# First chunks by pairs of input tiles, last job tile by tile, final stores on two queues

## The chip, the core and the metric

The kernel runs on one core of a Trainium2 chip. The metric is device time in microseconds (us) of one execution; shown are the median of several runs and one execution recorded by the hardware profiler. The engines are TensorE (PE for products, PEld for weight loads), VectorE (DVE), ScalarE (ACT), GpSimd (POOL) and SyncE (SP), which issues most DMAs.

## What is computed

One layer of a decoder trunk for 256 prompt tokens and 64 sample tokens (`NT` = 320 columns in all), width 2048, all in float32:

```python
x += 0.5 * SwiGLU_a(RMSNorm(x))    # w_ffa_in (2048 x 11264), w_ffa_out (5632 x 2048)
x += TokenMix(RMSNorm(x))          # mLSTM and dilated attention, w_in, w_pm, w_pa, w_out
x += 0.5 * SwiGLU_b(RMSNorm(x))    # w_ffb_in, w_ffb_out
y = RMSNorm(x)                     # final norm, written out for all tokens
```

Beside `y` the kernel returns attention rows and recurrent states; the change doesn't touch them.

## The kernel before

Activations are kept transposed: `X[j]` (j = 0 to 7) is a pair of tiles of 128 features by 320 tokens. Every matrix product is a job: 256 columns of a weight matrix, that is two halves `m` of 128, over all its input tiles. A job is cut into chunks of up to four input tiles, 512 KB of weights each. To keep float32 precision with faster products, a weight chunk `raw` is split into `hi` (ScalarE, line 223) and `lo` (VectorE, line 224), the moving operand likewise into `xh` and `xl`, and three products are summed in PSUM: `hi` by `xh`, `hi` by `xl`, `lo` by `xh` (line 144). `raw` has 4 buffers, `hi` and `lo` have 3 each.

The program order is written out by hand. `run_job` (line 270) goes through a job's chunks; ahead of each it splits chunks to come, takes one step of background generators (`every` at each chunk, `even` at every second), issues the loads to come, and then the chunk's products. Each engine works its instructions in this order. The evacuation of a job (`flush_evac`) runs in the first chunk of the next.

**Start.** The four `load_x` calls (512 columns of all tokens each, the prompt in one DMA and the sample tokens in another) alternate with the loads of weight chunks, all on SyncE's queue; six small vectors follow (`load_vecs`). `prep_pair(j)` (line 1494) transposes two 128-column tiles of x on TensorE, copies them to `X[j]`, and makes `XH[j]` (scaled, rounded) and `XL[j]` (the rest). `first_chunk` (line 1513) prepares pairs 0, 1 and 2 and splits chunk 0 ahead of the first product, with eight warming products on `ones`; the further pairs come between the halves of chunks 0 to 2. `first_sumsq` (line 1535) squares `X[0]` to `X[7]` on ScalarE in steps at chunks 2 to 5 and adds the squares into `ss` on VectorE (line 377); at chunk 6 `rstd_now` sums over features on TensorE (two products of `ones` by `ss`) and makes `rstd`, which the first evacuation needs. `init_tables` begins at the third chunk (its first `even` step comes at chunk 0 and only yields), `vec_table` at the fifth.

**End.** The last eight jobs make the final X pairs. `ffb_last` (line 1443) adds the job's result, squares it, scales by the final norm's weights (`xn`), and two chunks later transposes `xn` back and copies it into `Y` (128 x 3 x 2048). For the last job the sums over tokens (`token_sums`, line 1435) are taken in two parts, `ss` of pairs 0 to 6 during the job and `sq` of pair 7 behind it. Then `rt` (one factor a token) is made, and `Y` is scaled and stored in two halves of 1024 columns, three row tiles each (two of the prompt on 128 partitions, the sample rows on partitions 64 to 127), all six stores on SyncE's queue.

Of the kernel before, what the change touches and what calls it, by code (L numbers as in the profile page):

```python
# [128 lines left out]
def decoder_kernel(tc, I, O, K):  # L129
# [10 lines left out]
    def dma(out, in_):  # L140
        nc.sync.dma_start(out, in_)  # L141
# [128 lines left out]
    def run_job(job):  # L270
        cs, nkt, mov, evac, kind, setup = job
        ps = fg_tile()
        for n, (ci, k0, nk) in enumerate(cs):
            run_later()
            if ci < 5:
                first_chunk(ci, 0)
            else:
                split_upto(ci + HLB)
            if tick[0] % 2 == 0:
                step(even)  # L280
            else:
                step(odd)
            tick[0] += 1
            pace[0] += 8
            if pace[0] >= 15:
                pace[0] -= 15
                step(slow)
            step(every)
            if n == 0 and setup is not None:
                setup()  # L290
            if ci == 7 or (n == 0 and ci != 4):
                flush_evac()
            load_upto(ci + HLB + RAWB)
            h, l = wh.pop(ci), wl.pop(ci)
            for m in range(1 if kind == "mif" else 2):
                if m and ci < 3:
                    first_chunk(ci, 1)
                for k in range(nk):
                    xh, xl = mov(k0 + k)
                    if kind == "mif":  # L300
                        a, b, out = h[:, k], l[:, k], ps[0:64, 0, 0:NT]
                    else:
                        a, b, out = h[:, k, m * 128:(m + 1) * 128], l[:, k, m * 128:(m + 1) * 128], ps[:, m, 0:NT]
                    first, last = k0 + k == 0, k0 + k == nkt - 1
                    mm(out, a, xh, start=first, stop=False)
                    mm(out, a, xl, start=False, stop=False)
                    mm(out, b, xh, start=False, stop=last)
        pending[0] = (evac, ps)
# [58 lines left out]
                                   hi[:, m].bitcast(F32), op0=OP.mult, op1=OP.subtract)  # L367
        XH[j], XL[j] = hi, lo

    def sumsq(x, j, sq_pool):  # L370
        if j == 0:
            state["ss"] = sq_pool.tile([128, 2, NT], F32, tag="ss", bufs=1, name="ss")
            S.activation(state["ss"], x, AF.Square)
        else:
            sq = sq_pool.tile([128, 2, NT], F32, tag="ft", bufs=4, name="sq")
            S.activation(sq, x, AF.Square)
            V.tensor_tensor(state["ss"], state["ss"], sq, op=OP.add)

    def rstd_gen():
        yield  # L380
# [16 lines left out]
    X = {}  # L397
    S.dma_start(ident, K["ident"])
    vffa = fp.tile([16, 128], F32, name="vffa")
    S.dma_start(vffa, I["ln_ffa"].rearrange("o (k p) -> (o k) p", p=128))  # L400
    vrow = fp.tile([128, 2, 128], F32, name="vrow")
    xl = {}

    def load_x(c):
        xl[c] = fp.tile([128, 3, 512], F32, tag="xl", bufs=3, name="xl")
        G.memset(xl[c][64:128, 2], 0.0)
        dma(xl[c][:, 0:2], I["x_prompt"][0].rearrange("(t p) d -> p t d", p=128)[:, :, c * 512:(c + 1) * 512])
        dma(xl[c][0:NS, 2], I["x_sample"].rearrange("b t d -> (b t) d")[:, c * 512:(c + 1) * 512])

    def load_vecs():  # L410
        for r, nm in ((16, "ln_mix"), (32, "ln_ffb"), (48, "conv_b")):
# [989 lines left out]
    def ft_tile(name):  # L1401
        return pool_box["p"].tile([128, 2, NT], F32, tag="ft", bufs=4, name=name)
# [29 lines left out]

    TOK = (0, 128, NT - 128)

    def token_sums(x):
        ps = bg_tile()
        for t, t0 in enumerate(TOK):
            for m in range(2):
                mm(ps[:, t:t + 1], x[:, m, t0:t0 + 128], ones[:, 0:1], m == 0, m == 1)
        return ps  # L1440


    def ffb_last(ps, j):
        p = pool_box["p"]
        if j == 0:
            S.activation(epst2, epst, AF.Sqrt)
        if j < 7:
            V.scalar_tensor_tensor(X[j], ps[:, :, 0:NT], 0.5, X[j], op0=OP.mult, op1=OP.add)
            sumsq(X[j], j, p)
        else:  # L1450
            Y["sq"] = ft_tile("sq")
            for m in range(2):
                V.scalar_tensor_tensor(X[j][:, m], ps[:, m, 0:NT], 0.5, X[j][:, m], op0=OP.mult, op1=OP.add)
                S.activation(Y["sq"][:, m], X[j][:, m], AF.Square)
        xn = ft_tile("xn")
        for m in range(2):
            c = G_LF + 2 * j + m
            S.activation(xn[:, m], X[j][:, m], AF.Copy, scale=gv[:, c:c + 1])
        yield
        if j < 7:  # L1460
            yield
        if j == 6:
            pa_ = token_sums(state["ss"])
            V.tensor_copy(rt, pa_[:, 0:3])
        a, b = bg_tile(), bg_tile()
        for t in range(2):
            for m in range(2):
                tr(a[:, t * 256 + m * 128:t * 256 + (m + 1) * 128], xn[:, m, t * 128:(t + 1) * 128])
        for m in range(2):
            tr(b[:, m * 128:(m + 1) * 128], xn[:, m, NT - 128:NT])  # L1470
        if j == 0:
            Y["t"] = p.tile([128, 3, D], F32, name="Y")
        S.copy(Y["t"][:, 0:2, j * 256:(j + 1) * 256], a.rearrange("p (t c) -> p t c", t=2))
        V.tensor_copy(Y["t"][64:128, 2, j * 256:(j + 1) * 256], b[64:128, 0:256])

    ff_jobs(I["w_ffb_in"][0], I["w_ffb_out"][0], lambda: pool_box["p"], ffb_last)


    for c in range(4):
        load_x(c)  # L1480
        load_upto(c + 1)
    load_vecs()
    def warm(n):
        ps = bg_tile()
        for _ in range(n):
# [5 lines left out]
    tr(vps[:, 0:16], vffa)  # L1491
    V.tensor_copy(gv[:, 0:16], vps[:, 0:16])

    def prep_pair(j, fg=False):
        xv, c0, g0 = xl[j // 2], (j % 2) * 256, G_FFA + 2 * j
        X[j] = fp.tile([128, 2, NT], F32, tag="x", bufs=8, name="x")
        XH[j], XL[j] = t_tile(F32R, "xh"), t_tile(F32R, "xl")
        ft = fg_tile() if fg else None
        ps = [ft[:, 0], ft[:, 1]] if fg else [bg_tile(), bg_tile()]
        for m in range(2):  # L1500
            for t in range(2):
                tr(ps[m][:, t * 128:(t + 1) * 128], xv[:, t, c0 + m * 128:c0 + (m + 1) * 128])
            tr(ps[m][:, SEQ:SEQ + 128], xv[:, 2, c0 + m * 128:c0 + (m + 1) * 128])
        V.tensor_copy(X[j][:, 1], ps[1][:, 0:NT])
        for m in range(2):
            S.activation(XH[j][:, m], ps[m][:, 0:NT], AF.Copy, scale=gv[:, g0 + m:g0 + m + 1])
            if m == 0:
                S.copy(X[j][:, 0], ps[0][:, 0:NT])
        for m in range(2):
            V.scalar_tensor_tensor(XL[j][:, m], ps[m][:, 0:NT], gv[:, g0 + m:g0 + m + 1],  # L1510
                                   XH[j][:, m].bitcast(F32), op0=OP.mult, op1=OP.subtract)

    def first_chunk(n, m):
        if n == 0 and m == 0:
            prep_pair(0)
            prep_pair(1)
            split_upto(1)
            prep_pair(2, True)
            warm(8)
        elif n < 3:  # L1520
            prep_pair(2 * n + 2 + m)
            if m == 1:
                split_upto(n + 2)
        elif m == 0:
            split_upto(n + 2)

    def vec_table():
        for _ in range(4):
            yield
        vps = bg_tile()  # L1530
        tr(vps[:, 0:112], vrow[0:112, 0])
        tr(vps[:, 112:136], vrow[0:24, 1])
        V.tensor_copy(gv[:, 16:152], vps[:, 0:136])

    def first_sumsq():
        for c in ((), (), (0,), (1, 2), (3, 4, 5), (6, 7)):
            for j in c:
                sumsq(X[j], j, fp)
            yield
        rstd_now()  # L1540

    def init_tables():
        yield
        tab = fp.tile([128, TABW], F32, name="tab")
        dma(tab, K["tab"])
        rel = fp.tile([128, 8], F32, name="rel")
# [62 lines left out]
    spawn(first_sumsq())  # L1609
    spawn(vec_table())  # L1610
    spawn(init_tables(), even)
    for job in jobs:
        run_job(job)
    run_later()


    flush_evac()
    pb_ = token_sums(Y["sq"])
    V.tensor_tensor(rt, rt, pb_[:, 0:3], op=OP.add)
    S.activation(rt, rt, AF.Sqrt, bias=epst, scale=1.0 / D)  # L1620
    V.reciprocal(rt, rt)
    yt = Y["t"]
    ypv = O["y_prompt"][0].rearrange("(t p) d -> p t d", p=128)
    ysv = O["y_sample"].rearrange("b t d -> (b t) d")
    for c in range(2):
        if c:
            drain()
        for t in range(3):
            r0 = 0 if t < 2 else 64
            a = yt[r0:128, t, c * 1024:(c + 1) * 1024]  # L1630
            if t == 1:
                S.activation(a, a, AF.Copy, scale=rt[r0:128, t:t + 1])
            else:
                V.tensor_scalar(a, a, rt[r0:128, t:t + 1], None, op0=OP.mult)
            dma((ypv[:, t] if t < 2 else ysv)[:, c * 1024:(c + 1) * 1024], a)
    run_later(True)
    pool_box["es"].close()
    es.close()
# [31 lines left out]
```

## Time and profile before

| | |
|---|---|
| median of 3 runs | 2984.91 us (2981.57 to 2988.81) |
| profiled execution, its own time | 2990.0 us |
| its span, first to last instruction | 2988.2 us |
| mean granted TensorE clock | 0.992 |
| TensorE products busy | 2943.3 us, 98% of the span |
| VectorE, ScalarE, GpSimd busy | 1623.2, 1095.8, 218.8 us |
| moved by DMA | 556.97 MB, mean 186 GB/s |

Times below are microseconds from the span's start. `fg` is the PSUM tile of the jobs, `bg` that of all else. "L144" is line 144 of the kernel. Busy time says that an engine had work, not that the work was needed then; what sets the end is read from the chain of work that ended last and from the waits.

### The profile page before, as it was taken

The numbers are of one execution on the slowest core, as the hardware profiler recorded it, in microseconds if no ns is written. First come the engines' busy times: TensorE is split into PE (matmuls) and PEld (weight loads), VectorE is DVE, ScalarE is ACT, GpSimd is POOL, SyncE is SP. The second block draws the span as 40 slices with busy tenths as digits, with TensorE's granted clock in tenths as the row PEclk, the third lists the DMA queues.
The fourth block names the chain that finished last, engine by engine and source line by source line (L and its number), as shares of the span: only waits on it lengthen the run. The fifth ranks groups of instructions, "written<-read, shape, count | busy, mean of one in ns | idle before, by whom it ended". The sixth has DMA issues, their size and how long they took to land.

```text
span 2988.2 us, 49220 instructions
## 1 busy us (share of the span) xinstructions
PE 2943.3 (98%) x20514; PEld 2859.6 (96%) x20514; DVE 1623.2 (54%) x1865; ACT 1095.8 (37%) x1379; POOL 218.8 (7%) x233
## 2 busy tenths in 40 slices
PE   9999999999999999999899999999999999999998
PEld 8999999999999999888788998999999999999998
DVE  5444444444446556878777875655444444444444
ACT  5332333333334333434444443343333333333334
POOL 1000000000000000122222210000000000000000
PEclk9999999999999999999999999999999999999999
DMA  6454444444546788899999986554444444444443
GB/s 193 152 160 153 148 148 155 149 145 152 152 144 189 218 236 248 242 275 299 271 270 305 312 263 212 182 170 153 152 151 148 149 151 152 149 144 154 152 141 117
DMA packets 507461, 556.97 MB, mean 186 GB/s; under 512 B 30629, under 2 KB 452053, under 8 KB 507213
## 3 DMA queue, kind: packets, MB, share of 16 engines
q1 hardware_dynamic: 507060, 553.74, 60.1%
q8 instruction: 161, 2.64, 0.4%
q14 instruction: 64, 0.52, 0.1%
q10 hardware_dynamic: 176, 0.07, 0.0%
HBM read 521.45 MB, written 32.28 MB: 185 GB/s over the span
## 4 chain that ended last, share of the span: by engine, by line
PE 93%; DMA 4%; DVE 2%; SPq 1%; issue 1%; ACT 0%; POOL 0%; DVEq 0%; POOLq 0%; ACTq 0%
PE fg L144 87%; PE bg L144 5%; DMA vt<-in_cache_v_dram 1%; DMA raw<-in_w_in_dram 1%; PE bg L332 1%; SPq L141 1%; DVE lo L224 0%; DMA kraw<-in_cache_k_dram 0%; DMA k<-qk_d 0%; DMA xl<-in_x_sample_dram 0%; ACT hi L223 0%; DMA vq<-vm_d 0%; DVE kd L620 0%; DMA raw<-in_w_pm_dram 0%; DVE pre L965 0%
## 5 line engine op out<-in xcount | busy, mean ns | idle before, releaser
L224 DVE TENSOR_TENSOR lo<-raw,hi 128x1024 fp32r<-128x1024 f32 (+1 forms) x784 | 966.8, 1234 | 1222.4 <-ACT hi L223 1205.8
L144 PE MATMUL fg<-xh,hi 128*128 128x320 f32 x4240 | 1323.1, 312 | 0.3 <-ACT hi L223 0.3
L144 PE MATMUL fg<-xh,lo 128*128 128x320 f32 x4240 | 1313.2, 310 | 2.2 <-DVE lo L224 2.2
L144 PE MATMUL fg<-xl,hi 128*128 128x320 f32 x4240 | 1312.7, 310 | 0.0
L223 ACT CAST hi<-raw 128x1024 fp32r<-128x1024 f32 (+1 forms) x784 | 806.4, 1029 | 1373.3 <-PE fg L144 1034.1
L144 PEld LDWEIGHTS fg<-xh,hi 128*128 128x128 f32 x4240 | 797.4, 188 | 3.2 <-issue 1.3
L144 PEld LDWEIGHTS fg<-xh,lo 128*128 128x128 f32 x4240 | 796.9, 188 | 3.5 <-DVE lo L224 3.3
L144 PEld LDWEIGHTS fg<-xl,hi 128*128 128x128 f32 x4240 | 797.4, 188 | 0.9 <-issue 0.2
L144 PE MATMUL fg<-hh,hi 128*128 128x320 f32 x1408 | 437.1, 310 | 0.0
L144 PE MATMUL fg<-hh,lo 128*128 128x320 f32 x1408 | 435.3, 309 | 0.0
L144 PE MATMUL fg<-hl,hi 128*128 128x320 f32 x1408 | 435.3, 309 | 0.0
L144 PEld LDWEIGHTS fg<-hl,hi 128*128 128x128 f32 x1408 | 264.4, 188 | 0.7 <-issue 0.7
L144 PEld LDWEIGHTS fg<-hh,hi 128*128 128x128 f32 x1408 | 264.3, 188 | 0.7 <-issue 0.7
L144 PEld LDWEIGHTS fg<-hh,lo 128*128 128x128 f32 x1408 | 264.3, 188 | 0.0
L436 POOL TENSOR_TENSOR gt<-gt,rstd 128x640 f32<-128x640 f32 x44 | 69.2, 1573 | 1882.0 <-ACT gt L435 1882.0
L144 PE MATMUL fg<-bh,hi 128*128 128x320 f32 x512 | 160.3, 313 | 1.5 <-ACT bh L1338 1.5
L144 PE MATMUL fg<-bl,hi 128*128 128x320 f32 x512 | 159.9, 312 | 1.9 <-DVE bl L1339 1.9
L144 PE MATMUL fg<-bh,lo 128*128 128x320 f32 x512 | 159.6, 312 | 0.0
L620 DVE STREAM_TRANSPOSE kd<-kraw 128x512 f32<-128x512 f32 x160 | 102.1, 682 | 7.1 <-DMA kraw<-in_cache_k_dram 7.1
L144 PEld LDWEIGHTS fg<-bh,hi 128*128 128x128 f32 x512 | 97.2, 190 | 3.7 <-ACT bh L1338 2.0
L144 PEld LDWEIGHTS fg<-bl,hi 128*128 128x128 f32 x512 | 97.4, 190 | 2.4 <-DVE bl L1339 2.4
L144 PEld LDWEIGHTS fg<-bh,lo 128*128 128x128 f32 x512 | 97.3, 190 | 0.0
(299 smaller groups left out, 1484.5 us busy)
## 6 DMA issues: line engine op xcount, KB each, us to landing
raw<-in_w_ffa_in_dram SPq DMA_DIRECT2D x176, 512.0 KB
raw<-in_w_in_dram SPq DMA_DIRECT2D x176, 512.0 KB
raw<-in_w_ffb_in_dram SPq DMA_DIRECT2D x176, 512.0 KB
raw<-in_w_ffa_out_dram SPq DMA_DIRECT2D x80, 512.0 KB
raw<-in_w_ffb_out_dram SPq DMA_DIRECT2D x80, 512.0 KB
kraw<-in_cache_k_dram SPq DMA_DIRECT2D x96, 256.0 KB
vt<-in_cache_v_dram SPq DMA_DIRECT2D x128, 192.0 KB
kraw<-in_cache_k_dram SPq DMA_DIRECT2D x32, 512.0 KB
```

The costliest lines, as they stand in the source:

```text
L141: nc.sync.dma_start(out, in_)
L144: T.matmul(out, a, b, start=start, stop=stop, **kw)
L223: S.copy(hi[:, :nk], t[:, :nk])
L224: V.tensor_tensor(lo[:, :nk], t[:, :nk], hi[:, :nk].bitcast(F32), op=OP.subtract)
L332: T.transpose(out, in_, ident[:k, :k])
L436: G.tensor_tensor(gt, gt, bcast(rstd, 2), op=OP.mult)
L620: V.transpose(kd[:, 2 * pr + g], t[:, g])
```

## The change

At the start, the sample tokens of x tiles 0 to 2 are loaded on ScalarE's queue; on SyncE's queue x tile 0 and weight chunk 0 come in halves, alternating, then x 1, weights 1, x 2, weights 2 and 3, and, when a buffer is free, x 3. In each of the first four chunks the products go pair by pair (`hi` by `xh`, `hi` by `xl`, `lo` by `xh`, each for both halves `m`), and the pair after next is prepared in between; the weight split of these chunks goes by halves inside `prep_pair`, ahead of the copies to `X`. The eight warming products go. The adds of `first_sumsq` move to GpSimd. `load_vecs` moves to the ninth chunk and `vec_table`'s transposes to the thirteenth; `init_tables` begins at the thirteenth chunk.

At the end, `run_last` does the last job's two halves one after the other, each over all its chunks; the first half's squares, `xn`, three transposes and `Y` copies fall into the second half, whose second chunk also takes the sums of `ss` and of the first half. Behind the last product stand one half's add, square, three sums and three transposes. The last 128 columns of `Y` are scaled straight from PSUM. The second row tile's stores go to ScalarE's queue.

```diff
@@ run_job
-            if ci < 5:
-                first_chunk(ci, 0)
-            else:
+            if ci > 3:
                 split_upto(ci + HLB)
...
+            if ci < 4:
+                first_chunk(ci, ps)
+                load_upto(ci + 1 + RAWB)
+                continue
             load_upto(ci + HLB + RAWB)
...
-                if m and ci < 3:
-                    first_chunk(ci, 1)
@@ sumsq(x, j, sq_pool, eng=V)
-            V.tensor_tensor(state["ss"], state["ss"], sq, op=OP.add)
+            eng.tensor_tensor(state["ss"], state["ss"], sq, op=OP.add)
@@ start
-    for c in range(4):
-        load_x(c)
-        load_upto(c + 1)
-    load_vecs()
+    load_x(0, S)
+    S.dma_start(vffa, I["ln_ffa"].rearrange("o (k p) -> (o k) p", p=128))
+    load_x(1, S)
+    load_x(2, S)
+    raw[0] = wp.tile([128, 4, 256], F32, tag="raw", bufs=RAWB, name="raw")
+    for a in range(2):
+        load_xp(0, 256 * a, 256 * a + 256)
+        dma(raw[0][:, 2 * a:2 * a + 2], chunks[0][0][:, 2 * a:2 * a + 2])
+    st["loaded"] = 1
+    for c in (1, 2):
+        load_xp(c, 0, 512)
         load_upto(c + 1)
+    load_upto(4)
+    load_x(3)
+    load_xp(3, 0, 512)
...
+    def split_half(i, a):
+        if a == 0:
+            for d, nm in ((wh, "hi"), (wl, "lo")):
+                d[i] = wp.tile([128, 4, 256], F32R, tag=nm, bufs=HLB, name=nm)
+        r = slice(2 * a, 2 * a + 2)
+        S.copy(wh[i][:, r], raw[i][:, r])
+        V.tensor_tensor(wl[i][:, r], raw[i][:, r], wh[i][:, r].bitcast(F32), op=OP.subtract)
...
@@ prep_pair
-        V.tensor_copy(X[j][:, 1], ps[1][:, 0:NT])
...
+        split_half(j // 2, j % 2)
+        S.copy(X[j][:, 0], ps[0][:, 0:NT])
+        V.tensor_copy(X[j][:, 1], ps[1][:, 0:NT])
...
+    def first_chunk(n, ps):
+        if n == 0:
             prep_pair(0)
             prep_pair(1)
...
+        elif n == 3:
+            split_upto(5)
+        for pair in (2 * n, 2 * n + 1):
+            k0 = 2 * (pair % 2)
+            for which in range(3):
+                for m in range(2):
+                    for k in range(k0, k0 + 2):
...
+                        mm(ps[:, m, 0:NT], w, xl_ if which == 1 else xh, which == 0 and kt == 0, which == 2 and kt == 15)
+            if pair < 6:
+                prep_pair(pair + 2)
+            elif pair == 6:
+                split_upto(6)
...
@@ vec_table
+        for _ in range(8):
+            yield
+        load_vecs()
@@ first_sumsq
-                sumsq(X[j], j, fp)
+                sumsq(X[j], j, fp, G)
@@ init_tables
-        yield
+        for _ in range(6):
+            yield
@@ end
+    def run_last(job):
+        cs, nkt, mov, evac, kind, setup = job
+        for m in range(2):
+            ps = fg_tile()
+            for n, (ci, k0, nk) in enumerate(cs):
+                run_later()
+                split_upto(ci + HLB)
+                step(every)
+                if m == 0 and n == 0:
+                    flush_evac()
+                if m == 1 and n == 1:
+                    sp = token_sums([(state["ss"], 0), (state["ss"], 1), (Y["sq"], 0)])
+                    V.tensor_copy(rt, sp[:, 0:3])
+                    a = last_tr(0)
...
+            last_sum(ps, m)
...
-    for c in range(2):
-        if c:
-            drain()
+    drain()
+    for c0, c1, c2 in ((0, 1024, 1024), (1024, 1920, D)):
...
+            eng = S if t == 1 else nc.sync
...
+            if c2 > c1:
+                scale(y[:, c1:c2], a[r0:128, t * 128:(t + 1) * 128])
+            scale(y[:, c0:c1], y[:, c0:c1])
+            eng.dma_start((ypv[:, t] if t < 2 else ysv)[:, c0:c2], y[:, c0:c2])
```

`last_sum(ps, m)` is one half's add, square and `xn`; `last_tr(m)` its three transposes.

## Rows read from the trace of the kernel before

**Rows 1.** The page: span and number of instructions.

```profile
span 2988.2 us, 49220 instructions
```

**Rows 2.** Stretches of the start: busy us (instructions) of each engine, clock, DMA share, GB/s.

```profile
0.00:6.00 6.00, 4.33 (x21) 3.98 (x21) 0.17 (x1) 1.47 (x2) 1.87 (x9) 1.00 0.54 161
6.00:7.70 1.70, 1.35 (x11) 1.07 (x10) 0.56 (x2) 0.93 (x3) 0.00 (x0) 1.00 1.07 392
7.70:11.10 3.40, 1.05 (x9) 0.84 (x9) 2.88 (x6) 2.63 (x5) 0.52 (x1) 1.00 1.10 285
11.10:14.50 3.40, 3.40 (x18) 3.40 (x17) 2.06 (x4) 1.27 (x3) 0.00 (x0) 0.50 1.09 279
14.50:19.00 4.50, 4.50 (x35) 4.49 (x35) 1.70 (x4) 2.31 (x4) 0.00 (x0) 1.00 1.08 287
```

**Rows 3.** Timeline of TensorE's start: start, us, instruction, idle before it and releaser.

```profile
10.49 0.63 PE L332 MATMUL fg<-ident,xl 128*128 128x128 f32 x4 [0.28 <-DMA xl<-in_x_sample_dram]
...
14.10 0.58 PE L144 MATMUL fg<-xh,hi 128*128 128x320 f32 x1
```

**Rows 4.** The chain that ended last, 31 to 73 us: start, us, what.

```profile
31.75 3.49 PE fg L144 x22
...
42.26 0.84 DVE ss L377
...
43.23 1.31 PE bg L144 x4
44.54 28.16 PE fg L144 x192
```

**Rows 5.** Timeline of ScalarE: the kinds of instruction that the start has.

```profile
7.61 0.94 ACT L1506 ACTIVATE xh<-bg,gv 128x320 fp32r<-128x320 f32 x2
...
8.45 0.42 ACT L1508 COPY x<-bg 128x320 f32<-128x320 f32 x1
...
29.40 1.98 ACT L223 CAST hi<-raw 128x1024 fp32r<-128x1024 f32 x2
31.28 1.37 ACT L376 ACTIVATE sq<-x 128x640 f32<-128x640 f32 x2
...
2944.12 0.62 ACT L223 CAST hi<-raw 128x512 fp32r<-128x512 f32 x1 [0.89 <-ACT Y L1473]
```

**Rows 6.** Timeline of VectorE: the same.

```profile
16.99 0.49 DVE L1504 COPY x<-bg 128x320 f32<-128x320 f32 x1 [2.37 <-PE bg L332]
...
23.27 1.09 DVE L1510 SCALAR_TENSOR_TENSOR xl<-bg,gv,xh 128x320 fp32r<-128x320 f32 x2
...
34.41 1.22 DVE L224 TENSOR_TENSOR lo<-raw,hi 128x1024 fp32r<-128x1024 f32 x1
...
2944.77 0.69 DVE L224 TENSOR_TENSOR lo<-raw,hi 128x512 fp32r<-128x512 f32 x1 [0.30 <-ACT hi L223]
```

**Rows 7.** Timeline, 51.5 to 54 us, GpSimd beside VectorE.

```profile
51.91 1.57 POOL L436 TENSOR_TENSOR gt<-gt,rstd 128x640 f32<-128x640 f32 x1 [43.58 <-ACT gt L435]
52.73 1.83 DVE L224 TENSOR_TENSOR lo<-raw,hi 128x1024 fp32r<-128x1024 f32 x1 [1.74 <-ACT hi L223]
```

**Rows 8.** The chain that ended last, from 2970 us.

```profile
2970.14 1.23 PE bg L144 x12
2971.37 0.71 PE bg L332 x6
2972.09 1.77 PE fg L144 x12
...
2974.99 1.65 PE bg L144 x12
```

**Rows 9.** Stretches of the stores, columns as in rows 2.

```profile
2979.00:2981.50 2.50, 0.00 (x0) 0.00 (x0) 1.90 (x3) 1.16 (x2) 0.00 (x0) 0.50 1.03 405
2981.50:2983.25 1.75, 0.00 (x0) 0.00 (x0) 0.00 (x0) 0.00 (x0) 0.00 (x0) 0.50 0.97 206
2983.25:2986.75 3.50, 0.00 (x0) 0.00 (x0) 0.00 (x0) 0.00 (x0) 0.00 (x0) 0.50 0.98 357
```

More of the change, by code (lines that the diff above doesn't have):

```diff
@@ L368, in norm_in, with sumsq @@
         XH[j], XL[j] = hi, lo
-    def sumsq(x, j, sq_pool):
+    def sumsq(x, j, sq_pool, eng=V):
         if j == 0:
@@ L399, in decoder_kernel, with load_x, load_xp @@
     vffa = fp.tile([16, 128], F32, name="vffa")
-    S.dma_start(vffa, I["ln_ffa"].rearrange("o (k p) -> (o k) p", p=128))
     vrow = fp.tile([128, 2, 128], F32, name="vrow")
     xl = {}
-    def load_x(c):
+    xpr = I["x_prompt"][0].rearrange("(t p) d -> p t d", p=128)
+    xsm = I["x_sample"].rearrange("b t d -> (b t) d")
+    def load_x(c, eng=None):
         xl[c] = fp.tile([128, 3, 512], F32, tag="xl", bufs=3, name="xl")
         G.memset(xl[c][64:128, 2], 0.0)
-        dma(xl[c][:, 0:2], I["x_prompt"][0].rearrange("(t p) d -> p t d", p=128)[:, :, c * 512:(c + 1) * 512])
-        dma(xl[c][0:NS, 2], I["x_sample"].rearrange("b t d -> (b t) d")[:, c * 512:(c + 1) * 512])
+        (eng or nc.sync).dma_start(xl[c][0:NS, 2], xsm[:, c * 512:(c + 1) * 512])
+    def load_xp(c, c0, c1):
+        dma(xl[c][:, 0:2, c0:c1], xpr[:, :, c * 512 + c0:c * 512 + c1])
     def load_vecs():
@@ L1433, in decoder_kernel, with token_sums @@
     TOK = (0, 128, NT - 128)
-    def token_sums(x):
+    def token_sums(xs):
         ps = bg_tile()
         for t, t0 in enumerate(TOK):
-            for m in range(2):
-                mm(ps[:, t:t + 1], x[:, m, t0:t0 + 128], ones[:, 0:1], m == 0, m == 1)
+            for i, (x, m) in enumerate(xs):
+                mm(ps[:, t:t + 1], x[:, m, t0:t0 + 128], ones[:, 0:1], i == 0, i == len(xs) - 1)
         return ps
@@ L1446, in ffb_last @@
             S.activation(epst2, epst, AF.Sqrt)
[L1447 to L1454, printed above, removed]
+        V.scalar_tensor_tensor(X[j], ps[:, :, 0:NT], 0.5, X[j], op0=OP.mult, op1=OP.add)
+        sumsq(X[j], j, p)
         xn = ft_tile("xn")
@@ L1459, in ffb_last @@
         yield
-        if j < 7:
-            yield
-        if j == 6:
-            pa_ = token_sums(state["ss"])
-            V.tensor_copy(rt, pa_[:, 0:3])
+        yield
         a, b = bg_tile(), bg_tile()
@@ L1474, in ffb_last, with last_sum @@
         V.tensor_copy(Y["t"][64:128, 2, j * 256:(j + 1) * 256], b[64:128, 0:256])
-    ff_jobs(I["w_ffb_in"][0], I["w_ffb_out"][0], lambda: pool_box["p"], ffb_last)
-    for c in range(4):
-        load_x(c)
+    def last_sum(ps, m):
+        p = pool_box["p"]
+        if m == 0:
+            Y["sq"], Y["xn"] = ft_tile("sq"), ft_tile("xn")
+        x, c = X[7][:, m], G_LF + 14 + m
+        V.scalar_tensor_tensor(x, ps[:, 0, 0:NT], 0.5, x, op0=OP.mult, op1=OP.add)
+        S.activation(Y["sq"][:, m], x, AF.Square)
+        S.activation(Y["xn"][:, m], x, AF.Copy, scale=gv[:, c:c + 1])
@@ new lines, in last_tr @@
+    def last_tr(m):
+        xn, a = Y["xn"], bg_tile()
+        for t, t0 in enumerate(TOK):
+            tr(a[:, t * 128:(t + 1) * 128], xn[:, m, t0:t0 + 128])
+        return a
+    def run_last(job):
[12 more added lines that the diff above has]
+                    a = last_tr(0)
+                    S.copy(Y["t"][:, 0:2, 1792:1920], a[:, 0:256].rearrange("p (t c) -> p t c", t=2))
+                    V.tensor_copy(Y["t"][64:128, 2, 1792:1920], a[64:128, 256:384])
+                for k in range(nk):
+                    xh, xl = mov(k0 + k)
+                    c = slice(m * 128, (m + 1) * 128)
+                    first, last = k0 + k == 0, k0 + k == nkt - 1
+                    mm(ps[:, 0, 0:NT], wh[ci][:, k, c], xh, first, False)
+                    mm(ps[:, 0, 0:NT], wh[ci][:, k, c], xl, False, False)
+                    mm(ps[:, 0, 0:NT], wl[ci][:, k, c], xh, False, last)
+            last_sum(ps, m)
@@ L1492, in decoder_kernel, with prep_pair @@
     V.tensor_copy(gv[:, 0:16], vps[:, 0:16])
-    def prep_pair(j, fg=False):
+    def split_half(i, a):
[5 more added lines that the diff above has]
+        V.tensor_tensor(wl[i][:, r], raw[i][:, r], wh[i][:, r].bitcast(F32), op=OP.subtract)
+        if a == 1:
+            raw.pop(i)
+            st["split"] = i + 1
+    def prep_pair(j):
         xv, c0, g0 = xl[j // 2], (j % 2) * 256, G_FFA + 2 * j
@@ L1497, in prep_pair @@
         XH[j], XL[j] = t_tile(F32R, "xh"), t_tile(F32R, "xl")
-        ft = fg_tile() if fg else None
-        ps = [ft[:, 0], ft[:, 1]] if fg else [bg_tile(), bg_tile()]
+        ps = [bg_tile(), bg_tile()]
         for m in range(2):
@@ L1503, in prep_pair @@
             tr(ps[m][:, SEQ:SEQ + 128], xv[:, 2, c0 + m * 128:c0 + (m + 1) * 128])
-        V.tensor_copy(X[j][:, 1], ps[1][:, 0:NT])
         for m in range(2):
             S.activation(XH[j][:, m], ps[m][:, 0:NT], AF.Copy, scale=gv[:, g0 + m:g0 + m + 1])
-            if m == 0:
-                S.copy(X[j][:, 0], ps[0][:, 0:NT])
         for m in range(2):
@@ L1511, in prep_pair @@
                                    XH[j][:, m].bitcast(F32), op0=OP.mult, op1=OP.subtract)
-    def first_chunk(n, m):
-        if n == 0 and m == 0:
+        split_half(j // 2, j % 2)
[3 more added lines that the diff above has]
+        if n == 0:
             prep_pair(0)
             prep_pair(1)
[L1517 to L1525, printed above, removed]
+        elif n == 3:
[5 more added lines that the diff above has]
+                    for k in range(k0, k0 + 2):
+                        kt = 4 * n + k
+                        xh, xl_ = mov_x(kt)
+                        w = (wl if which == 2 else wh)[n][:, k, m * 128:(m + 1) * 128]
+                        mm(ps[:, m, 0:NT], w, xl_ if which == 1 else xh, which == 0 and kt == 0, which == 2 and kt == 15)
[3 more added lines that the diff above has]
+                split_upto(6)
+        wh.pop(n)
+        wl.pop(n)
     def vec_table():
+        for _ in range(8):
+            yield
+        load_vecs()
         for _ in range(4):
@@ L1542, in init_tables @@
     def init_tables():
-        yield
+        for _ in range(6):
+            yield
         tab = fp.tile([128, TABW], F32, name="tab")
@@ L1611, in decoder_kernel @@
     spawn(init_tables(), even)
-    for job in jobs:
+    for job in jobs[:-1]:
         run_job(job)
+    run_last(jobs[-1])
     run_later()
-    flush_evac()
-    pb_ = token_sums(Y["sq"])
-    V.tensor_tensor(rt, rt, pb_[:, 0:3], op=OP.add)
+    sp = token_sums([(Y["sq"], 1)])
+    a = last_tr(1)
+    V.tensor_tensor(rt, rt, sp[:, 0:3], op=OP.add)
     S.activation(rt, rt, AF.Sqrt, bias=epst, scale=1.0 / D)
@@ L1624, in decoder_kernel, with scale @@
     ysv = O["y_sample"].rearrange("b t d -> (b t) d")
-    for c in range(2):
-        if c:
-            drain()
+    drain()
+    for c0, c1, c2 in ((0, 1024, 1024), (1024, 1920, D)):
         for t in range(3):
             r0 = 0 if t < 2 else 64
[L1630 to L1635, printed above, removed]
+            y = yt[r0:128, t]
+            eng = S if t == 1 else nc.sync
+            def scale(out, in_):
+                if t == 1:
+                    S.activation(out, in_, AF.Copy, scale=rt[:, 1:2])
+                else:
+                    V.tensor_scalar(out, in_, rt[r0:128, t:t + 1], None, op0=OP.mult)
+            if c2 > c1:
+                scale(y[:, c1:c2], a[r0:128, t * 128:(t + 1) * 128])
+            scale(y[:, c0:c1], y[:, c0:c1])
+            eng.dma_start((ypv[:, t] if t < 2 else ysv)[:, c0:c2], y[:, c0:c2])
     run_later(True)
```

## The prediction

> **What bounds the kernel now.** I read the page first for the span [rows 1], then the chain that ended last, because only what stands on it can give time. Between 44.54 and 72.70 us that chain is 192 matmuls into `fg` in 28.16 us without a gap, 0.147 us each [rows 4]: in steady state TensorE's own stream is the time, and nothing in this change shortens that stream (the same number of products, with the same tiles). So the change can only act at the two ends, and there I read the timeline, then the stretches.
>
> At the start, TensorE issues its first weight product at 14.10 us; before that it stands 0.28 us for the second sample tile, which has landed by 10.4 us [rows 3]. Meanwhile the DMA engines are the full resource: busy share over 1 from 6 us on, 279 to 392 GB/s [rows 2]. At 35.24 us the first four chunks are done, and the sum of squares is turned into `rstd` by products that start at 43.23 us [rows 4]; from there the stream doesn't break. At the other end, the last weight product ends at 2973.86 us, the sums that the final scale needs end at 2976.64 us [rows 8], and the stores then fill the DMA engines from 2979 to 2986.75 us [rows 9].
>
> **The start: first product.** The changed queue asks for the same bytes in another order: the sample tiles on ScalarE's queue, on SyncE's queue x half, weight half, x half, weight half, then whole tiles. I take the rate of the trace as it is. Bytes moved (rate by time) are 966 KB by 6.0 us, 1,632 by 7.7, 2,601 by 11.1, 3,550 by 14.5, 4,842 by 19 [rows 2]. The lag from last byte to use comes from the second sample tile: identity, scale vector, two x tiles and one weight tile are 1,909 KB, moved by 8.7 us, used at 10.49, so 1.75 us. In the new order the second x half has ahead of it the identity, vector, three sample tiles, x half and weight half: 1,253 KB with itself, moved by 6.7 us, landed at 8.5. By the same sum: second weight half 9.2, x tile 1 at 10.9, weight tile 1 at 12.7, x tile 2 at 14.6, weight tiles 2 and 3 at 16.5 and 18.3, x tile 3 at 20.6.
>
> TensorE's order is: transposes of pairs 0 and 1, the 12 products of pair 0, transposes of pair 2, products of pair 1, and so on. Six transposes take 0.71 us [rows 8], twelve products 1.76. So products begin at 8.5 + 0.7 = 9.25 us, 4.85 earlier than now, and a pair costs 2.47 us. The landings meet this: pair 2's transposes stand at 11.0 (needs 10.9), pair 4's at 15.9 (14.6), pair 6's at 20.9 (20.6). The other engines do too: per pair ScalarE has 0.94 + 0.42 + 0.62 = 1.98 us, VectorE 1.09 + 0.49 + 0.69 = 2.27 [rows 5, 6], both under 2.47. The `bg` buffers of a pair now come free only behind the half split, but its last copy ends some 2.7 us after its transposes and the buffers are wanted two pairs, 4.9 us, later. The eight warming products on `ones`, which now stand between the transposes of 10.49 and the first weight product [rows 3], go. Pairs 6 and 7 follow without transposes, and the four chunks end at 9.25 + 6 x 2.47 + 2 x 1.76 = 27.6 us against 35.24: 7.6 us won so far.
>
> **The start: what is late next.** Two things take some of it back. First the split of chunk 4. ScalarE reaches pair 7 at 23.8 us and has 0.94 + 0.62 + 0.42, then two squares 1.37, then this cast 0.99 (two take 1.98 [rows 5]): 28.1 us; VectorE's `lo` ends at 29.4, and TensorE, which wants it for its third product at 27.9, waits 1.5 us. Second the sum of squares. Its seven adds move from VectorE to GpSimd. No such add on GpSimd is in the trace; the nearest row, a product of the same shape, takes 1.57 us [rows 7]; VectorE's add takes 0.84 on the chain [rows 4]. In that place both engines ran: GpSimd's 1.57 us ended 0.75 us into VectorE's `lo`, which took 1.83 in place of 1.22 [rows 6, 7]. So an add lies between 0.84 and, if next time GpSimd pays those 0.6 us, 2.2. I take 1.57, the same engine and shape, and 0.6 more for `lo`. The first square is ready at 26.4, two adds end at 29.6; the third square stands on ScalarE behind the casts of chunks 4, 5 and 6 (28.1 + 2 x 0.99 + 0.7 = 30.8 us); five adds then end at 38.65. TensorE arrives at the `rstd` products at 27.9 + 1.5 + 0.6 + 22 x 0.147 + 3.52 = 36.7 us and waits 1.9. The `rstd` products start at about 38.6 instead of 43.23: 4.6 us remain of 7.6.
>
> **The clock.** At 11.1 to 14.5 us the granted clock is 0.50, 1.2 GHz, after a stretch in which TensorE was busy 1.05 of 3.4 us [rows 2]; now only the warming products pay for it. In the new order weight products run there, and TensorE has waits ahead of pair 1 (about 1.5 us) and again in chunks 4 to 6. One such 3.4 us stretch costs 1.7 us of products. I charge 1.2 us for two possible ones, between 0 and 3.4, part of each falling into a wait anyway.
>
> **Moved and free.** The six small vector loads go from 10 to 18 us to the ninth chunk, the tables from the third chunk to the thirteenth, with all their issues on SyncE and their later TensorE and VectorE steps ten chunks on. They stand there between weight loads whose ring is four deep; the unbroken 28.16 us is the cover [rows 4], and without it each would cost its issue time. Their readers come hundreds of chunks later: nothing.
>
> **The tail.** The last job's two halves run one after the other, so the first half's square sum and three transposes go into the second half's stream. Ahead of the last product this adds six more records of sums (1.23 us for twelve [rows 8]) and half of 0.71 us: 0.62 + 0.36 = 0.98 us later. Behind it, the way to the sums stays at 1.13 us (2973.86 to 2974.99), and the sums shrink from 1.65 to 0.62: 1.03 us. So `rt` is ready when it is now; only the second half's stores gain, since their `Y` copies go. But those stores wait for the engines: 405 GB/s, then 206 for 1.75 us while the sample rows go alone, then 357 [rows 9]. All 2.62 MB at 405 would take 6.5 us of the 7.75, so the second queue is worth between 0 and 1.2 us. I take 0.5, as the last sample store still ends alone.
>
> The Trainium skill ("DMA: Bandwidth & Descriptors", section "Issuing engines are not separate DMA queues") says that transfers started by several engines share the same 16 DMA engines and that only issue time is saved; by it alone the tail gives 0 and the sum ends 0.5 us higher. The busy share near 1 in both store stretches agrees with it.
>
> **Sum.** 4.6 - 1.2 + 0.5 = 3.9 us. The profiled run had a span of 2988.2 and a time of 2990.0; it becomes 2986.1. The median of the runs shown is 2984.91, so I predict 2981.0.
>
> **Rivals.**
> - GpSimd isn't waited for (22%): the squares come early enough, or an add costs nearer 0.84. Then `rstd` starts when TensorE gets there, at 36.1 or a little before; 7.1 to 7.6 us at the start, little clock loss, 0.5 at the tail: about 2977.5. For it: ScalarE has 0.5 us a pair to spare, so squares could run early. Against: they are issued behind pair 7's copy and three casts.
> - The loads are late (20%): the half tiles are fetched in 1 KB rows where x now moves in 2 KB rows, and the sample loads take their share of the same engines at once. Each microsecond on the second x half moves all behind it; 2 to 4 us late leaves 0 to 2 us: about 2984.
> - Slower (5%): GpSimd's adds, beside VectorE's splits, stretch themselves instead of `lo`. Five stand in a row on the path; the gain is gone when one takes 1.57 + 3.9 / 5 = 2.35 us, and at 3.6 us the kernel loses 6 us: about 2991. Against: the one such row, which took its 1.57 beside a split [rows 7].
>
> **Numbers.** Forecast (2 to 6 us won, 2979 to 2983) 50%, with 3% for anything else. 0.2% is 6 us, about what a measurement of this kernel can tell from no change. Faster by more: the first rival and the upper edge of the forecast, 27%. Slower by more: 6%. Within: 67%. The range goes from a first rival with a full tail, 2975.5, to late loads with a low clock, 2986.0.
>
> **What would show it.** Right: first weight product near 9.3 us; the fourth chunk's end near 27.6; a wait of TensorE for `lo` in chunk 4 of 1 to 2 us; a wait of the `rstd` products for GpSimd's `ss`; these products at 37.5 to 40 us; the end of the sums 1.8 us behind the last weight product, now 2.8; stores some 7 us long. Wrong: TensorE waiting for x or weight tiles in pairs 2 to 7, a clock of 0.50 in chunks 0 to 6 for more than one stretch, no wait for GpSimd, or new waits behind 44 us where the moved tables land.

## The result, and the profile after

The changed kernel takes 2989.94 us (median of 20 runs, 2980.59 to 2995.42) against 2984.41 us of the kernel before (20 runs): ratio 1.0017, 95% interval 1.0012 to 1.0023, that is 3.6 to 6.9 us slower. Predicted were 2981.0 us and a range of 2975.5 to 2986.0.

The profiled execution of the changed kernel is one of its shorter ones (2987.34 us), that of before one of its longer ones (2990.0), so their spans (2985.6 and 2988.2) don't rank the kernels. What ranks them is where each stands at a fixed instruction. I use two marks. The first is the first norm split of the mixer part (line 366); by then nearly a third of the span is over and only the start can have moved it:

```profile
L366 DVE SCALAR_TENSOR_TENSOR xl<-x,gv,xh x32: 543/549/553, 905.3 to 2038.1; 128x320 fp32r<-128x320 f32 x32
```

The columns are the shortest, median and longest duration in ns, then the first and the last start. In the kernel before the first start is 902.5: the start has lost 2.8 us.

```profile
L366 DVE SCALAR_TENSOR_TENSOR xl<-x,gv,xh x32: 544/549/554, 902.5 to 2041.6; 128x320 fp32r<-128x320 f32 x32
```

The second is the last split of the hidden activations, before and after:

```profile
L446 DVE TENSOR_TENSOR hl<-hf,hh x44: 824/826/828, 56.1 to 2900.3; 128x640 fp32r<-128x640 f32 x44
```

```profile
L449 DVE TENSOR_TENSOR hl<-hf,hh x44: 824/826/827, 58.4 to 2896.8; 128x640 fp32r<-128x640 f32 x44
```

From there to the span's end it is 87.9 us before and 88.8 after, so the end has lost 0.9. Between line 366's first and last start lie 1139.1 us before and 1132.8 after, in code that no edit touches; over all kernels below this stretch runs from 1131.9 to 1141.3 whatever was edited, and it is what makes single executions unfit to compare.

Timeline of TensorE's waits at the start, changed kernel (start, us, instruction, idle before it and releaser):

```profile
7.02 0.20 PE L332 MATMUL bg<-ident,vffa 16*128 16x16 f32 x1 [2.30 <-DMA vffa<-in_ln_ffa_dram]
...
28.64 0.41 PE L144 MATMUL fg<-xh,hi 128*128 128x320 f32 x1 [0.22 <-ACT hi L223]
29.90 0.41 PE L144 MATMUL fg<-xh,lo 128*128 128x320 f32 x1 [0.70 <-DVE lo L224]
42.94 2.50 PE L144 MATMUL bg<-ss,ones 128*128 128x320 f32 x4 [6.02 <-POOL ss L377]
```

From 7.2 to 28.6 us TensorE never waits for a tile; the four chunks are done some 7 us earlier than in [rows 4]. Then it arrives at the `rstd` products at 36.9 us and stands 6.02 us for GpSimd's `ss`. The chain of the same kernel shows the pairs and the adds:

```profile
9.69 2.50 PE fg L144 x12
12.18 0.66 PE bg L332 x6
12.84 1.76 PE fg L144 x12
...
27.17 1.58 POOL ss L377
28.75 0.07 issue
28.82 2.47 POOL ss L377
...
38.88 2.40 POOL ss L377
41.28 0.07 issue
41.35 1.54 POOL ss L377
42.89 0.04 issue
42.94 2.50 PE bg L144 x4
45.44 22.55 PE fg L144 x144
```

An add takes 1.54 to 1.58 us where no split of VectorE is under way when it starts, and 2.40 to 2.47 where one is. VectorE pays too, four splits in 8.78 us, 2.2 each in place of 1.22 [rows 6]:

```profile
28.62 8.78 DVE L224 TENSOR_TENSOR lo<-raw,hi 128x1024 fp32r<-128x1024 f32 x4 [1.43 <-ACT hi L223]
```

The clock, in the columns of rows 2: low for 3.4 us from 7.5 on, and again for 6.8 us, from late in the wait on:

```profile
7.70:11.10 3.40, 3.40 (x16) 3.15 (x15) 2.64 (x6) 3.18 (x8) 0.52 (x1) 0.53 1.07 304
...
36.00:41.60 5.60, 0.91 (x7) 0.65 (x5) 3.41 (x2) 2.33 (x2) 5.37 (x4) 1.00 0.68 205
41.60:48.40 6.80, 5.46 (x16) 4.68 (x17) 2.15 (x1) 0.53 (x1) 1.28 (x1) 0.50 0.18 62
48.40:55.00 6.60, 6.60 (x46) 6.60 (x46) 1.96 (x2) 3.98 (x4) 0.83 (x1) 0.99 0.17 49
```

The first low stretch isn't shown to have a price. The first twelve products took 2.50 us here in place of 1.76, but in the run "the start alone" below they took 3.16 us at a granted clock of 1.00.

So the `rstd` products start 0.3 us earlier than before [rows 4], but they take 2.50 us at 1.2 GHz in place of 1.31, and the stream behind them starts at the low clock: from `rstd` to the mark are 862.4 us, where the kernel before has 859.3. That difference of 3.1 less the 0.3 is the start's loss.

The end: the chain of the changed kernel, to be read against [rows 8],

```profile
2962.44 0.91 ACT xn L1454 x2
2963.35 0.04 issue
2963.40 0.76 PE bg L332 x5
2964.16 2.63 PE fg L144 x18
2966.79 1.90 PE bg L144 x18
2968.70 0.39 PE bg L332 x3
2969.08 2.65 PE fg L144 x18
...
2972.80 0.84 PE bg L144 x6
```

and the stretches of its stores, against [rows 9]:

```profile
2975.90:2978.40 2.50, 0.00 (x0) 0.00 (x0) 1.94 (x5) 1.30 (x2) 0.00 (x0) 0.74 0.97 387
2978.40:2980.10 1.70, 0.00 (x0) 0.00 (x0) 0.00 (x0) 0.00 (x0) 0.00 (x0) 0.50 1.01 219
2980.10:2983.70 3.60, 0.00 (x0) 0.00 (x0) 0.00 (x0) 0.00 (x0) 0.00 (x0) 0.50 0.98 352
```

From the last hidden split to the last weight product it is 74.9 us (73.6 before), from there to the end of the sums 1.9 (2.8), from there to the span's end 12.0 (11.6; over all kernels below 11.6 to 12.0 with the new end and some 11.5 with the old). The stores still take 7.8 us, with the slow stretch of the sample rows in the middle.

### The profile page after: what moved, and what is told of

Same layout as the page of the kernel before. It is cut to its first block, busy times and chain, and to the rows that moved or that the text cites. A ratio compares the mean times of both kernels' runs of the same rounds, so it can differ in the third digit from the quotient of the medians.

```text
span 2985.6 us, 49211 instructions
## 1 busy us (share of the span) xinstructions
PE 2940.3 (98%) x20498; PEld 2857.8 (96%) x20498; DVE 1622.0 (54%) x1864; ACT 1095.7 (37%) x1384; POOL 233.1 (8%) x240
## 4 chain that ended last, share of the span: by engine, by line
PE 95%; DMA 2%; DVE 1%; POOL 1%; issue 0%; ACT 0%; SPq 0%; ACTq 0%; DVEq 0%; POOLq 0%
PE fg L144 88%; PE bg L144 5%; PE bg L332 1%; POOL ss L377 0%; DMA raw<-in_w_in_dram 0%; DVE kd L623 0%; DMA vt<-in_cache_v_dram 0%; SPq L141 0%; DMA C<-in_state_C_dram 0%; DMA vq<-vm_d 0%; DMA raw<-in_w_pm_dram 0%; DVE lo L224 0%; DMA vffa<-in_ln_ffa_dram 0%; DMA kraw<-in_cache_k_dram 0%; DVE pre L968 0%
```

## The experiments

Theory A: GpSimd's adds, stretched by VectorE's splits, hold the `rstd` products, and the low clock behind that wait takes the rest of the start's gain. Theory B: the pair order and half loads cost the time themselves, and the adds fill a wait that would be there. For the end: its own added work, or the stores. "Mark" is the first start of line 366 (902.5 before, 905.3 changed), "end" the stretch from the last hidden split to the span's end (87.9, 88.8). The first four ran on one chip beside 33 runs of the kernel before (2985.85 us), the two of the better start beside 21 (2984.71 us). The other five were run once for their profile (2987.37 to 2992.53 us), and only their marks and rows are read.

**Adds back on VectorE.**

```diff
-                sumsq(X[j], j, fp, G)
+                sumsq(X[j], j, fp)
```

> The changed kernel with the seven adds of the squares back on VectorE; all else as changed. Marks: the rstd products (43.23 us before, 42.94 changed) and the first norm split of the next layer part (902.5 us before, 905.3 changed). Theory A (GpSimd's adds, at 2.4 us beside VectorE's splits, hold the rstd products, and the clock falls behind that wait): rstd products at 36 to 38 us, no low clock near 41 us, mark at 896 to 898, time 3 to 6 us under the kernel before. Rival B (the pair order and the half loads lose the time themselves, the adds only fill a wait that is there anyway): rstd products still after 41 us, mark at 902 or later, time not under the kernel before.

Measured: 2981.57 us (11 runs), ratio 0.9988 (0.9979 to 0.9997); mark 896.9, end 88.5. The chain:

```profile
36.14 0.84 DVE ss L377
...
37.11 1.32 PE bg L144 x4
38.43 21.12 PE fg L144 x144
```

One edit turns a slower kernel into a faster one: `rstd` 5.8 us earlier, no low clock (1.00 from 36 to 48.4 us). Theory B is out; the start without GpSimd is worth 5.6 us.

**The same edit alone, in the kernel before.**

```diff
-                sumsq(X[j], j, fp)
+                sumsq(X[j], j, fp, G)
```

> The kernel before with one edit, the seven adds of the squares on GpSimd. Theory A: the adds run beside VectorE's splits from about 32 us on, 7 times some 2.2 us, so the rstd products wait to 46 to 48 us (43.23 before), a low clock follows, mark at 906 to 910, time 4 to 8 us over the kernel before. Rival B: the adds hide, rstd products within 1 us of 43.23, mark within 1 us of 902.5, time as before.

Measured: 2992.07 us (11 runs), ratio 1.0022 (1.0013 to 1.0031); mark 908.1, end 87.9; the `rstd` products at 47.16 after a wait of 4.84 us for `ss`, taking 2.40 us, with a low clock at 47.3:

```profile
44.71 2.40 POOL ss L377
47.11 0.04 issue
47.16 2.40 PE bg L144 x4
```

The adds cost 5.6 us there (`rstd` 3.9 later, and 1.6 behind it) and 905.3 - 896.9 = 8.4 in the changed start (5.8 and 2.6).

**The start alone, the end alone.** The changed kernel with the old functions of the end, and the other way round (`token_sums`, `ffb_last`, `run_last` and the stores).

> The changed start with the old end. If the end costs about 1 us as the two traces say: mark at 905.3 as in the changed kernel, the stretch from the last hidden split (2900.3 before, 2896.8 changed) to the span's end 87.9 as before (88.8 changed), time 2 to 4 us over the kernel before. If the end were worth the 0.5 us that the prediction gave it: that stretch over 88.8, time over that of the changed kernel.

> The old start with the changed end. If the end costs about 1 us: mark at 902.5, last stretch 88.8, time 1 us over the kernel before (not to be told from none by time alone). If the end gains 0.5: last stretch 87.4.

Measured, start alone: 2989.18 us, ratio 1.0015 (1.0006 to 1.0024), mark 905.6, end 87.7. End alone: 2987.75 us, ratio 1.0002 (0.9993 to 1.0012), mark 903.1, end 88.6. The two losses are separate: 3.1 us sit in the start and 0.7 in the end, the latter below what the time can tell. A mark of one kernel is good to about 1 us: kernels with the same start as the changed one have it at 904.7 to 905.6, and 902.5 and 903.1 belong to one start too.

**Why 2.4 us.** In the changed kernel, VectorE's splits of chunks 4 to 8 become zeros, which read nothing (those products leave out their `lo` part); in a second one the add reads half of the square twice by a broadcast, as the product of [rows 7] reads `rstd` (the sum leaves out the other half).

```diff
+                if 4 <= i <= 8:
+                    V.memset(lo[:, :nk].bitcast(F32), 0.0)
...
-            eng.tensor_tensor(state["ss"], state["ss"], sq, op=OP.add)
+            eng.tensor_tensor(state["ss"], state["ss"], bcast(sq[:, 0], 2) if eng is G else sq, op=OP.add)
```

> The changed kernel with VectorE's splits of chunks 4 to 8 replaced by zeros (those chunks leave out the lo product's part), so that VectorE reads nothing from SBUF beside GpSimd's adds. If the two engines' reads contend: every add near 1.55 us, the rstd products at 37 to 39 us, mark under 900. If an add with two full operands takes 2.4 us on GpSimd by itself: adds stay at 2.4, rstd products at 42 to 43 us.

> The changed kernel, in which each GpSimd add reads one half of the square twice by a broadcast (so the sum leaves out the other half), as the gate product that took 1.57 us beside a split does with rstd. If the broadcast operand is what spared that product: adds near 1.6 us beside the splits, the splits near 1.8 us, rstd products at 37 to 39 us. If it was only that less of it lay beside a split: adds at 2.4 us as in the changed kernel, rstd products near 43 us.

GpSimd's instructions from 20 to 50 us, without the splits (busy, mean ns):

```profile
L380 POOL TENSOR_TENSOR ss<-ss,sq 128x640 f32<-128x640 f32 x7 | 10.9, 1564 | 17.8 <-ACT sq L379 17.4
```

with the broadcast, the splits in place:

```profile
L377 POOL TENSOR_TENSOR ss<-ss,sq 128x640 f32<-128x640 f32 x7 | 15.2, 2177 | 17.3 <-ACT sq L376 16.8
```

and VectorE's splits of that kernel, 27 to 40 us:

```profile
L224 DVE TENSOR_TENSOR lo<-raw,hi 128x1024 fp32r<-128x1024 f32 x5 | 10.8, 2205 | 1.9 <-ACT hi L223 1.9
```

So 2.4 us is no price of the add: beside an engine that only writes it takes 1.56, and the broadcast spares nothing. Without the splits the `rstd` products start at 39.58 us, after a wait of 3.5 us, and the clock is low behind that too (mark 901.8; 37 to 39 us and a mark under 900 were expected): 1.56 us an add is still too slow to hide. With the broadcast they start at 42.02 us.

What sets the price is which engine starts first. The sixth add of the changed kernel starts behind a split that is under way. It lies beside it for 1.00 us only, and is still stretched (lines of the timeline):

```profile
37.88 2.00 DVE L224 TENSOR_TENSOR lo<-raw,hi 128x1024 fp32r<-128x1024 f32 x1 [0.47 <-ACT hi L223]
38.88 2.39 POOL L377 TENSOR_TENSOR ss<-ss,sq 128x640 f32<-128x640 f32 x1
```

An add of the kernel before with its adds on GpSimd starts 0.18 us ahead of a split, lies beside it for 1.35 of its 1.53 us, and keeps its time; there the split pays:

```profile
43.10 1.53 POOL L377 TENSOR_TENSOR ss<-ss,sq 128x640 f32<-128x640 f32 x1
...
43.28 2.43 DVE L224 TENSOR_TENSOR lo<-raw,hi 128x1024 fp32r<-128x1024 f32 x1 [1.68 <-ACT hi L223]
```

The rows fit one rule: the later one stands until the earlier one has ended, and then takes nearly its own time (here the add has 1.39 us left behind the end of the split at 39.88, the split 1.08 behind the end of the add at 44.63). In the seven kernels here with adds on GpSimd and all splits in place, each of the 35 adds that start inside a split takes 2.10 to 2.46 us. Every other add and gate product, in all kernels here, takes 1.53 to 1.59, whatever part of it lies beside a split.

**The low clock.** 14 warming products ahead of the `rstd` products of the changed kernel.

```diff
+        warm(14)
         rstd_now()
```

> The changed kernel with 14 warming products on ones ahead of the rstd products, in the wait for GpSimd's adds. If the low clock behind that wait is a cost of its own: rstd products start where they did (41 to 44 us) but take 1.3 us in place of 2.5, no low clock at 40 to 50 us, mark 2 to 3 us under the changed kernel's 905.3. If the wait alone is the cost: mark within 0.7 us of it.

Measured: `rstd` products at 42.37 us in 1.51 us, mark 903.7. The warming products fill half of the wait (2.87 us are left); the low stretch shrinks from 6.8 to 3.4 us and moves to 43.4, and from `rstd` to the mark it is 861.3 us in place of 862.4. That gain of 1.1 us isn't shown to come from the warming: with the same 6 us wait and no warming the way from `rstd` to the mark is 861.2 to 862.4 us over five kernels. "The start alone" has the lowest, and its chain and the warmed one read

```profile
44.41 2.50 PE bg L144 x4
46.91 21.36 PE fg L144 x144
```

```profile
42.37 1.51 PE bg L144 x4
43.88 22.51 PE fg L144 x144
```

that is 23.86 and 24.02 us, against 25.05 in the changed kernel and 22.44 with the adds on VectorE. That the clock is a cost of its own, these five kernels show. Each has one low stretch of 6.8 us, but only 2.9 to 5.5 us of it lie behind the start of the `rstd` products. The way to the mark is 1.4 to 2.6 us longer than the 859.8 with the adds on VectorE, in each case about half of that part.

**The end's parts.** All six stores on SyncE's queue; and the transposes of the last pair but one a step later.

```diff
-            eng = S if t == 1 else nc.sync
+            eng = nc.sync
...
         yield
         yield
+        if j == 6:
+            yield
```

> The changed kernel with all six final stores on SyncE's queue. If the second queue saves only issue time that the busy DMA engines hide anyway: the stretch from the end of the last sums to the span's end (11.95 us changed, 11.56 before) within 0.4 us of the changed kernel's. If it lets the stores overlap: 0.5 to 1.2 us longer.

> The changed kernel with the transposes of the last pair but one a step later, in the last job's second half. If they are what holds the end (six transposes that took 1.22 us in place of 0.82, waiting for xn): last stretch (from the last hidden split to the span's end) 88.3 to 88.5 in place of 88.8. If the end costs only what it adds in sums: 88.8.

Measured: with one queue the stretch from the end of the sums (2978.89) to the span's end (2990.7) is 11.8 us, end 88.7: the second queue is worth nothing that shows. With the late transposes the end is 88.2, 0.6 less than in the changed kernel, and the six transposes take 0.66 us without a wait. Up to the last weight product, the part that they can change, it is 74.5 us, against 74.9 to 75.0 in all other kernels with the new end: they are worth some 0.5 us.

**A start that beats both kernels.** Adds on VectorE with the old end; and the same with the scale vector's load ahead of the first sample tile and 11 warming products in place of 9.

```diff
-    load_x(0, S)
     S.dma_start(vffa, I["ln_ffa"].rearrange("o (k p) -> (o k) p", p=128))
+    load_x(0, S)
...
-    warm(9)
+    warm(11)
```

> The changed start with the adds on VectorE, and the old end. If start and end add up as measured alone: mark near 897 us (902.5 before), last stretch 87.9 us, time 5 to 6 us under the kernel before, ratio near 0.998. If the end change is worth something in company: time not under that of the run with the adds on VectorE (ratio 0.9988).

> The run before it with the scale vector's load ahead of the first sample tile on ScalarE's queue and two more warming products. If the late vector (transposes from 7.0 us in the changed kernel, 5.5 before) holds the start: first weight product 0.5 to 1.5 us earlier, mark at 895.5 to 896.5, time 0 to 1.5 us less. If the x half's landing holds it: no move of the first product.

Measured: 2980.73 us, ratio 0.9989 (0.9980 to 0.9997), mark 897.4, end 87.8; and 2980.40 us, ratio 0.9985 (0.9976 to 0.9994), mark 896.7, end 87.8. The first is 4.0 us under the kernel before, less than the 5 to 6 expected. The second's two edits move the first weight product from 9.8 to 8.9 us; the mark moves by 0.7, little more than the 0.5 by which it differs between the two other kernels with this start and the adds on VectorE. The time tells neither apart. The last one is 4.3 us under the kernel before, as far as the changed kernel with the adds on VectorE alone; the old and the new end can't be ranked by time.

## Why the prediction was wrong

**What held.** The first product: 9.25 predicted, 9.69 measured, with the vector's landing (7.02) and not the second x half as the last to come. That this comes so near is in part luck: behind the vector came 13 transposes that took 2.66 us together, where the sum had six in 0.7 behind an x half at 8.5. With the vector loaded first TensorE does wait for that x half, until 8.24, and the first product follows at 8.91. The pair's 2.47 us: 2.42 (0.66 + 1.76). No wait for a tile in pairs 2 to 7. The end of the four chunks: 27.6 predicted, 28.4 (28.64 less the wait of 0.22). TensorE's arrival at the `rstd` products: 36.7 predicted, 36.9. The stretched split of chunk 4: a 1.5 us wait predicted, and some 0.9 in two pieces measured. And that `rstd` waits for GpSimd was in the sum.

**The step that failed** is the price of an add: "I take 1.57, the same engine and shape, and 0.6 more for `lo`." The mechanism, five adds in a row on the path, was right; of these five, four took 2.39 to 2.45 us and the last 1.53. With the gaps they ran for 11.5 us in place of 7.85, from 31.36 instead of 30.8 on. That moves `rstd` from the 38.6 predicted by 4.3 us to 42.94. What came out is nearest to the slower rival, with the difference that `lo` is stretched as well; its turning point of 2.35 us an add isn't reached by the five's mean of 2.24, and the rest of the loss lies in the clock and the end. The row that the price came from [rows 7] showed both engines together for 0.75 us of GpSimd's 1.57, and there VectorE alone was stretched; I read from it that GpSimd never is. But in that row GpSimd had started first. In the start of the changed kernel five adds start behind a split that is under way, and four splits start behind one of these adds, so both engines are stretched in turn. Neither the broadcast operand nor the length of the overlap is the reason.

**The clock** was charged 1.2 us for two stretches, and this term was too small as well. The late one came with the wait, which was three times as long as predicted: the whole way from `rstd` to the mark grew by 3.1 us, of which the run with the adds on VectorE took back 2.6. Of the 0.5 that stays, 0.27 are the two transposes of `vec_table`, moved from ahead of the `rstd` products to behind them. It wasn't the add's price alone: in the run without the splits an add takes 1.56, as I had counted, and yet the wait is 3.5 us and not 1.9, the way to the mark is 862.2, and the mark, 901.8, is only 0.7 us better than before, where 3.4 were predicted for the start.

**The end** was given a gain of 0.5 us and loses 0.9. The sum of the parts: the stream ahead of the last product is 1.4 us longer, not 0.98, as the pair before the last is now transposed half as many products after its evacuation, before its `xn` is there (some 0.5 us, shown by moving it); from the last product to the end of the sums 0.9 is won, not 1.03; and the second queue gives nothing, where the prediction took 0.5 between bounds of 0 and 1.2. The last 0.4, from the sums to the span's end, no run takes apart. The Trainium skill's rule, which stood beside that term ("DMA: Bandwidth & Descriptors", section "Issuing engines are not separate DMA queues"), agrees with the trace: the busy share is 0.97 to 1.03 in both kernels' store stretches, and one queue or two makes no difference that shows.

**The sum.** At the marks the start misses its forecast by 6.2 us (4.3 at `rstd`, 3.1 behind it, less the 1.2 charged) and the end by 1.4, 7.6 together: 3.9 us won were predicted, 3.7 lost are seen there.

**What stays open.** The marks give 2.8 + 0.9 = 3.7 us, the medians 5.5 (3.6 to 6.9). The rest, if it is one, lies in the middle stretch, whose length varies by 9 us among all profiles here; no run separates it. The granted clock goes with that length: in the middle stretch it stands at 1.2 GHz for 17 to 24 us in the six shortest (up to 1135.9 us) and for 27 to 31 us in the seven others.

## What to carry to other kernels

An engine's price for an instruction is read from a row in the company it will have: a duration that was measured alone, or where the instruction started first, bounds it from below when it will start behind an instruction of the other engine. So look at the order of the two starts, and not only at the overlap. Work that is taken off a busy engine and put on an idle one is free only while nothing waits for its last result; here the sum of squares had 10 us until TensorE came for it and took 16. And where a gain is taken ahead of a fixed meeting point, look first at who else has to come to that point.

## What was not expected of the hardware

GpSimd's add of 128x640 and VectorE's split of 128x1024 make each other wait, and the one that starts later pays: the add goes from 1.56 to 2.4 us, the split from 1.22 to as much as 2.6. The one that starts first keeps its time, even with 1.35 of 1.53 us side by side. Five traces of the same 6 us wait at TensorE show 1.4 to 2.6 us more lost behind it, by how much of a stretch of 6.8 us at 1.2 GHz fell behind the wait.
